# Rolling a matrix by DMA: row copies in long DMAs of shrinking size instead of one row per engine

## The chip, the cores and the metric

The kernel runs on one core of a Trainium2 chip. The metric is the device time of one execution in microseconds (us), the median of several runs. Jobs differ: the median of the kernel before lay between 818 and 832 us in the jobs below (831.87 and 820.19 us in two jobs that both name chip 9), so every comparison is with runs of the kernel before on the same chip in the same rounds.

## The reference

```python
x = np.random.randn(8192, 8192).astype(np.float32)      # 256 MiB
def reference(x, shift):                                 # shift = 100
    return np.roll(x, shift, axis=1)
```

Every row moves 100 columns to the right, and its last 100 elements come to the front. It is a copy: 268.44 MB have to be read from HBM and as much written.

## The kernel before

The output's columns 256 to 8191 (the *rows*, 31,744 bytes each) are copied straight from HBM to HBM, by the issuing queues of SP and ACT in turn. The first 256 columns (the *heads*) go through SBUF, on GpSimd's queue, with two VectorE copies per tile that put the wrapped pieces together.

```python
engines = [nc.sync, nc.scalar]
xm = x.rearrange("(c e j) w -> c j e w", e=16, j=4)
om = out.rearrange("(c e j) w -> c j e w", e=16, j=4)
for c in range(n_rows // 64):              # 128 blocks of 64 rows
    for j in range(4):                     # one row for each of the 16 DMA engines
        engines[j % 2].dma_start(out=om[c, j, :, a:], in_=xm[c, j, :, g:n_cols - s])
# ... heads: 20 loads of HBM into SBUF on GpSimd's queue, 8 VectorE copies ...
for k, h in enumerate(tiles):
    for q in range(Q):
        nc.gpsimd.dma_start(out=ot[k, q, :, :, :a], in_=h[:, q])      # 16 stores
```

Here `s` is 100, `a` is 256 and `g` is 156. Each row DMA gives one row to each engine. The framework keeps four DMAs per issuing queue in flight: the fifth is issued when the first has landed on all 16 engines.

Of the kernel before, what the change touches and what calls it, by code (L numbers as in the profile page):

```python
# [1 line left out]

# [4 lines left out]


@with_exitstack
def kernel(  # L10
    ctx: ExitStack,
    tc: tile.TileContext,
    x: bass.AP,
    shift: int,
    out: bass.AP,
):
    nc = tc.nc
    n_rows, n_cols = x.shape
    s = shift % n_cols
    a = -(-s // 128) * 128  # L20
    if 0 < a <= 384 and a + 128 <= n_cols:
        a += 128
    g = a - s
    P = nc.NUM_PARTITIONS
    engines = [nc.sync, nc.scalar]
    n_chunks = 16
    rows = n_rows // n_chunks





    xm = x.rearrange("(c e j) w -> c j e w", e=16, j=4)
    om = out.rearrange("(c e j) w -> c j e w", e=16, j=4)
    if a < n_cols:
        for c in range(n_rows // 64):
            for j in range(4):
                engines[j % 2].dma_start(out=om[c, j, :, a:], in_=xm[c, j, :, g:n_cols - s])
    if a == 0:
        return  # L40


    if a > 512:
        for i in range(n_chunks):
            r = slice(i * rows, (i + 1) * rows)
            nc.gpsimd.dma_start(out=out[r, :s], in_=x[r, n_cols - s:])
            if g > 0:
                nc.gpsimd.dma_start(out=out[r, s:a], in_=x[r, :g])
        return





    Q, J = 4, 4
    n_st = n_rows // (P * Q * J)
    reads = ctx.enter_context(tc.tile_pool(name="reads", bufs=n_st))
    heads = ctx.enter_context(tc.tile_pool(name="heads", bufs=n_st))
    xt = x.rearrange("(k p j q) c -> k q p j c", q=Q, j=J, p=P)
    ot = out.rearrange("(k p j q) c -> k q p j c", q=Q, j=J, p=P)  # L60
    tiles = []
    for k in range(n_st):
        t = reads.tile([P, Q - 1, J, a], x.dtype)
        h = heads.tile([P, Q, J, a], x.dtype)
        for q in range(1, Q):
            lead = bass.AP(tensor=x.tensor, offset=(k * P * J * Q + q) * n_cols - s,
                           ap=[[J * Q * n_cols, P], [Q * n_cols, J], [1, a]])
            nc.gpsimd.dma_start(out=t[:, q - 1], in_=lead)  # L68
        nc.gpsimd.dma_start(out=h[:, Q - 1, :, :s], in_=xt[k, Q - 1, :, :, n_cols - s:])  # L69
        nc.vector.tensor_copy(h[:, :Q - 1, :, :s], t[:, :, :, :s])  # L70
        if g > 0:
            nc.gpsimd.dma_start(out=h[:, 0, :, s:], in_=xt[k, 0, :, :, :g])  # L72
            nc.vector.tensor_copy(h[:, 1:, :, s:], t[:, :, :, s:])  # L73
        tiles.append(h)
    for k, h in enumerate(tiles):
        for q in range(Q):
            nc.gpsimd.dma_start(out=ot[k, q, :, :, :a], in_=h[:, q])  # L77


# [1 line left out]
_INS = ['x', 'shift']  # L81
_OUTS = [((8192, 8192), 'float32')]

_NUMBERS = {'shift': 100}


# [26 lines left out]
```

## Time and profile before

| | |
|---|---|
| time, median of 3 runs | 821.17 us (819.21 to 822.31) |
| profiled span | 818.3 us |
| share of the engines' time in packets: q1, q10, q0 | 46.0%, 46.4%, 6.8% |
| HBM traffic over the span | 656 GB/s |
| row DMAs, size, time to landing | 512, 496 KB, 12.6 us |
| last head packet over at | 484.9 us |

Whether the 16 DMA engines are the bound, or wait inside their packets for something shared, has to be read from the packets' durations. The prediction does this and shows the lines. In them, a row of 40 digits or numbers stands for 40 equal slices of the span; a digit is the engines' busy share in tenths (9 is 90% or more).

### The profile page before, as it was taken

To read this page: it belongs to the slowest core of one execution; us is meant where nothing else is said; L and a number is where in the kernel's file an instruction comes from. 1 tells how busy PE (TensorE), PEld (TensorE's weight loads), DVE (VectorE), ACT (ScalarE), POOL (GpSimd) and SP (SyncE) were. 2 spreads that over 40 slices of the span, in tenths; PEclk is the share of its full clock that TensorE was granted. 3 is DMA by queue.
4 is the path that set the end of the run, shared out by engine and by line. 5 is a ranking of instruction groups with operands and counts; after the bars stand their busy time and mean duration, and the time that the engine had idled before them with its cause. 6 is when DMAs were issued, how large, how long until landed. Compare 5 with 4: busy or idle time off the path is not lost. (4 is left out here: it accounts for less than half of the span.)

```text
span 818.3 us, 617 instructions
## 1 busy us (share of the span) xinstructions
DVE 7.7 (1%) x8; POOL 28.8 (4%) x40
## 2 busy tenths in 40 slices
DVE  0000000000000000000000000000000000000000
POOL 3000000000000000000000000000000000000000
DMA  9999999999999999999999999999999999999997
GB/s 313 343 345 352 338 352 342 363 338 358 349 342 352 354 355 352 348 364 357 337 335 341 327 335 334 326 332 334 338 337 334 330 334 334 332 327 334 334 321 262
DMA packets 21060, 276.89 MB, mean 338 GB/s; under 512 B 8768, under 2 KB 8768, under 8 KB 12864
## 3 DMA queue, kind: packets, MB, share of 16 engines
q10 hardware_dynamic: 8192, 130.04, 46.4%
q1 hardware_dynamic: 8192, 130.04, 46.0%
q0 software_dynamic: 4672, 16.78, 6.8%
q14 instruction: 4, 0.03, 0.0%
HBM read 268.44 MB, written 268.44 MB: 656 GB/s over the span
## 5 line engine op out<-in xcount | busy, mean ns | idle before, releaser
L77 POOL DMA_DIRECT2D out_dram<-h x16 | 13.2, 825 | 197.8 <-DMA out_dram<-h 112.6
L68 POOL DMA_DIRECT2D t<-in_x_dram x12 | 9.5, 793 | 59.7 <-DMA h<-in_x_dram 30.0
L70 DVE COPY h<-t 128x1200 f32<-128x1200 f32 x4 | 3.1, 786 | 232.3 <-DMA t<-in_x_dram 173.4
L73 DVE COPY h<-t 128x1872 f32<-128x1872 f32 x4 | 4.9, 1224 | 0.0
L69 POOL DMA_DIRECT2D h<-in_x_dram x4 | 3.0, 748 | 45.4 <-DMA t<-in_x_dram 45.4
L72 POOL DMA_DIRECT2D h<-in_x_dram x4 | 3.0, 750 | 41.7 <-DMA t<-in_x_dram 41.7
L94 POOL MEMSET const-float32-0.0<- 128x1 f32 x1 | 0.1, 98 | 0.2 <-issue 0.2
L94 POOL MEMSET const-bfloat16-1.0<- 128x1 bf16 x1 | 0.1, 102 | 0.0
L94 POOL MEMSET const-uint8-127<- 128x1 uint8 x1 | 0.1, 99 | 0.0
L94 POOL MEMSET const-float32-1.0<- 128x1 f32 x1 | 0.1, 98 | 0.0
## 6 DMA issues: line engine op xcount, KB each, us to landing
out_dram<-in_x_dram ACTq DMA_DIRECT2D x256, 496.0 KB, 12.6
out_dram<-in_x_dram SPq DMA_DIRECT2D x256, 496.0 KB, 12.6
out_dram<-h POOLq DMA_DIRECT2D x16, 512.0 KB, 113.7
t<-in_x_dram POOLq DMA_DIRECT2D x12, 512.0 KB, 94.9
h<-in_x_dram POOLq DMA_DIRECT2D x4, 312.0 KB, 92.1
h<-in_x_dram POOLq DMA_DIRECT2D x4, 200.0 KB, 97.4
```

The lines of the kernel that those rows point to most:

```text
L68: nc.gpsimd.dma_start(out=t[:, q - 1], in_=lead)
L69: nc.gpsimd.dma_start(out=h[:, Q - 1, :, :s], in_=xt[k, Q - 1, :, :, n_cols - s:])
L70: nc.vector.tensor_copy(h[:, :Q - 1, :, :s], t[:, :, :, :s])
L72: nc.gpsimd.dma_start(out=h[:, 0, :, s:], in_=xt[k, 0, :, :, :g])
L73: nc.vector.tensor_copy(h[:, 1:, :, s:], t[:, :, :, s:])
L77: nc.gpsimd.dma_start(out=ot[k, q, :, :, :a], in_=h[:, q])
L94: nc = _bacc.Bacc("TRN2", target_bir_lowering=False, num_devices=1)
```

## The change

Its intent is fewer and larger row DMAs. A DMA now holds up to 32 rows per engine; the sizes shrink (32, 24, 18, 13, 10, 7, 6, 4, 3, 2, 2, then 1) so that the end stays fine-grained, and the last four blocks are cut in half rows.

```diff
-    xm = x.rearrange("(c e j) w -> c j e w", e=16, j=4)
-    om = out.rearrange("(c e j) w -> c j e w", e=16, j=4)
-    if a < n_cols:
-        for c in range(n_rows // 64):
-            for j in range(4):
-                engines[j % 2].dma_start(out=om[c, j, :, a:], in_=xm[c, j, :, g:n_cols - s])
+    xm = x.rearrange("(c e j) w -> j e c w", e=16, j=4)
+    om = out.rearrange("(c e j) w -> j e c w", e=16, j=4)
+    blocks = n_rows // 64
+    steps, c = [], 0
+    while c < blocks:
+        steps.append((c, max(1, (blocks - c) // 4)))
+        c += steps[-1][1]
+    for c, n in steps:
+        ways = 2 if c >= blocks - 4 else 1
+        edge = [a + (n_cols - a) * k // ways for k in range(ways + 1)]
+        for j in range(4):
+            for lo, hi in zip(edge, edge[1:]):
+                if lo < hi:
+                    engines[j % 2].dma_start(out=om[j, :, c:c + n, lo:hi], in_=xm[j, :, c:c + n, lo - s:hi - s])
```

The heads' code is the same in both.

## The prediction

> **What bounds the kernel now.** I read the page's slices first, to see which engine is full. Compute is all but idle (VectorE 7.7 us, GpSimd 28.8 us of 818.3), while the row of the DMA engines is full from the first slice to the last but one:
>
> ```profile
> DMA  9999999999999999999999999999999999999997
> GB/s 313 343 345 352 338 352 342 363 338 358 349 342 352 354 355 352 348 364 357 337 335 341 327 335 334 326 332 334 338 337 334 330 334 334 332 327 334 334 321 262
> ```
>
> The reader is to see two stages: some 350 GB/s up to slice 19, some 333 GB/s from slice 20 on, and a short fall at the end. Next, the queues and the memory:
>
> ```profile
> q10 hardware_dynamic: 8192, 130.04, 46.4%
> q1 hardware_dynamic: 8192, 130.04, 46.0%
> q0 software_dynamic: 4672, 16.78, 6.8%
> ...
> HBM read 268.44 MB, written 268.44 MB: 656 GB/s over the span
> ```
>
> q1 and q10 carry the rows (columns 256 to 8191, 31,744 bytes each), q0 carries the heads. Together 99.2% of the 16 engines' time is packets: there is almost no empty time to win. What has to shrink is the time of a packet itself. Third, the stretches of time:
>
> ```profile
> 200.00:300.00 100.00, 1.83 (x2) 6.60 (x8) 1.00 1.01 349
> ...
> 500.00:600.00 100.00, 0.00 (x0) 0.00 (x0) 1.00 1.00 333
> 600.00:700.00 100.00, 0.00 (x0) 0.00 (x0) 1.00 1.00 334
> 700.00:800.00 100.00, 0.00 (x0) 0.00 (x0) 1.00 1.00 329
> 800.00:818.00 18.00, 0.00 (x0) 0.00 (x0) 1.00 0.73 258
> ```
>
> The last column is GB/s through the DMA engines, the one before it their busy share. A row is read from HBM and written to HBM, so from 500 us on HBM sees 2 x 333 = 666 GB/s. From 200 to 300 us the packet records have 4.31 MB of heads, 43 GB/s, which touch HBM only once: 2 x (349 - 43) + 43 = 655 GB/s. Two different mixes, the same HBM traffic within 2%: I take HBM, near 660 GB/s, to be the bound, and not the engines.
>
> The packet records of the trace support this. A row's packet took 1,467 ns in the mean (6,016 + 6,077 us of the two queues, less 74 us of small packets, over 8,192 rows), but never less than 1,173 ns, and about a fifth took 1,173 to 1,180 ns. That floor is 31,744 B / 1.175 us = 27.0 GB/s per engine, 432 GB/s for 16. When engines run out of work at the end, so that 9 or fewer are still busy (after 812 us), every row takes 1,174 to 1,175 ns. With all 16 at work the mean is 1,513 ns. So a row is stretched because the others are there: a shared limit.
>
> Last, the waits of the issuing queue and the issues:
>
> ```profile
> SPq L38 <- DMA out_dram<-in_x_dram: 670.4, 252, 3.9
> ...
> out_dram<-in_x_dram ACTq DMA_DIRECT2D x256, 496.0 KB, 12.6
> out_dram<-in_x_dram SPq DMA_DIRECT2D x256, 496.0 KB, 12.6
> out_dram<-h POOLq DMA_DIRECT2D x16, 512.0 KB, 113.7
> ```
>
> SP waits 252 times out of 256 issues: the first four go out free, each later one waits for the one four before it. So four DMAs per queue, eight rows per engine, are in flight. 670 us of waiting look large but cost nothing, since the engines stay full behind them. The last head packet is over at 484.9 us, 330 us before the end: the heads are off the end's path.
>
> **What the Trainium skill says.** (1) "DMA: Bandwidth & Descriptors", section "Anatomy of one DMA": about 2 us fixed cost per DMA, mostly waiting for the write's receipt, while the semaphore write itself is nearly free. The trace agrees on the second: a completion packet takes 9 ns, and in the bulk-only stretch (490 to 812 us) a row right after completion packets takes 1,512 ns, a row after another row 1,513 ns. (2) The same page, "Queues, rings and completion order": each engine goes round its queues packet by packet. The trace agrees: on an engine a q1 row, a q10 row, and their two completion packets follow each other. (3) The same page, "Rules for kernel authors": at least 1 MiB per DMA for full bandwidth. The rows' DMAs have 496 KB, so the rule speaks for the change; the full engines speak against a gain from it. (4) "HBM Reference", "Specifications (TRN2)": 716 GB/s per HBM domain. The 656 GB/s of this trace are 92% of that.
>
> **The change part by part.** The instruction order shows 44 row DMAs on each of SP and ACT in place of 256: for each of the four row residues j, DMAs of 32, 24, 18, 13, 10, 7, 6, 4, 3, 2, 2 rows per engine, then seven of one row, of which the last four are cut in two halves. GpSimd's and VectorE's lists are the same, so the heads are untouched. Bytes are the same; the descriptors stay one row of 31,744 B, but for 16 rows per engine that become two halves. On an engine the rows are still the 512 rows e x 4 + j of each 64-row block, only in another order.
>
> *Removed: completion packets.* 512 x 16 = 8,192 become 88 x 16 = 1,408. On an engine, q1 row and q10 row abut (the next starts 2 ns before the end), and across the two completion packets the next row starts about 8 ns after the end: a pair costs about 10 ns. 256 pairs: 2.6 us per engine; 83% of it goes, 2.1 us. This is worth its full size only if engines are the bound. Under an HBM bound other rows stretch into it: I count a third, 0.7 us.
>
> *Removed: issues.* 424 issues at 510 to 517 ns are 108 us of sequencer time per queue, all beside full engines: 0 us.
>
> *Moved: the end.* Following each engine's packets by their times, the 16 engines stop between 811.2 and 816.8 us, mean 813.7. Perfect balance would gain 3.1 us. With half rows the last steps in flight are half as long: I count half, 1.5 us, less a little because HBM is less loaded when few engines run (rows at 1,175 rather than 1,513 ns): 1.2 us.
>
> *Moved: how far engines may part.* Now the 16 completions of a DMA come within about 6 us of each other (at most 9.3), since a fifth DMA waits for the slowest engine. With 32 rows per DMA, an engine may lead by dozens of rows. In the first 60 us of the run the spread grew from 0.6 to 5.9 us before it stopped growing, so engines do part. Every engine has the same 512 rows, so a leader stops early or is held back in the small steps, and the laggards then run at the floor. This costs nothing as long as about 12 engines are at work (12 x 27 x 2 = 648 GB/s). I count 0, with an uncertainty of a per cent or so, because another set of rows open at once may suit HBM better or worse.
>
> *Added: descriptor generation of long DMAs.* 512 descriptors in an issue instead of 16. The engine starts on the first while the rest are made: 0 to 1 us at the start.
>
> Sum: 0.7 + 1.2 + 0 - 0.5 = about 1.4 us less, 820. I lean a little further, to 817, because of the two open terms (completions, row order) the first can only gain, up to 1.4 us more, and a change of this shape was presumably kept for a reason.
>
> **Rivals.** *Completions do cost.* If the 292 ns by which the mean row exceeds the floor (1,467 - 1,175) came from one completion per row, long DMAs would remove most of it: 512 x 0.29 = 150 us per engine. HBM at the stated 716 GB/s would stop it at 536.9 MB / 716 = 750 us. For it: 496 KB DMAs and the rule of 1 MiB. Against it: rows after completions are no longer than others, and lone engines with completions run at the floor. 8%, giving 750 to 790 us.
>
> *Row order and HBM.* Stretches come from a shared limit, and that may depend on which rows are open together. In the first 5 us, when engines were still in step, the second row took 1,251 to 1,298 ns on all 16, faster than ever later with 16 at work. So the way the streams lie to each other can matter. With engines further apart it may go either way: 800 to 835 us. 20% for a visible effect.
>
> *The heads starve.* If an engine took a whole DMA of 32 rows as one turn, heads would get one packet per 64 rows, about 95 us, and would be left for the end. Their packets are 890 us in sum, 56 us per engine (41 at the floor, 256 x 160 ns), with the chain read, copy, write behind: 840 to 860 us. The present trace can't exclude it, as each DMA has one row per engine. But a row of 31,744 B is a packet by itself here, and 4 pieces of 1,024 B make one of 4,096 on q0: packets go by size, and I expect rows to stay packets. 5%.
>
> **Range and chances.** The main path gives 815 to 821 us. HBM's reaction widens it to 800 to 828, which should hold 8 times in 10. More than 2% faster means under 804.7: most of the 8% of the first rival, and about a third of the second: 0.15. More than 2% slower means over 837.6: the starving heads and a little of the second: 0.07. The rest, 0.78, is the same.
>
> **What would show it.** Right: completions on q1 and q10 fall from 4,096 to 704 each, the engines' share stays near 99%, HBM stays within 1% of 656 GB/s, rows in the bulk-only stretch stay near 1,500 ns with the same floor, heads still end by 500 us, the last engines stop within some 4 us. Wrong: rows' mean falls toward 1,175 ns (completions or order did cost), rows grow longer (order), the q0 packets run to the end of the span (starving), or engines are empty in the last slices by more than now (they parted and were not brought together). A time under 800 or above 828 would mean that the shared limit is not the fixed 660 GB/s that I read.

## The result

The changed kernel took 825.36 us (823.34 to 826.5, six runs) against 820.99 us (818.13 to 822.31, six runs) for the kernel before. The ratio is 1.0058, with a 95% interval of 1.0037 to 1.0079. A ratio is the mean time of one kernel's runs over that of the other's of the same rounds, so not quite the ratio of the medians. The change costs 0.6%: inside the predicted range, but a loss where a small gain was forecast.

The page of the changed kernel, slices and queues (queue, packets, MB, share of the 16 engines' time):

```profile
DMA  9999999999999999999999999999999999899988
GB/s 312 329 341 343 343 338 342 341 336 336 336 344 341 333 347 341 342 329 345 341 335 338 339 332 344 338 342 340 350 343 343 334 333 342 332 355 339 316 278 301
...
q10 hardware_dynamic: 4928, 130.03, 45.7%
q1 hardware_dynamic: 4928, 130.03, 44.8%
q0 software_dynamic: 4672, 16.78, 7.1%
HBM read 268.44 MB, written 268.44 MB: 651 GB/s over the span
```

Two things are new. The sharp step at slice 20 is gone: the heads, which made it, no longer end there. And the engines are no longer full near the end: the shares add up to 97.6% of a longer span, and the last slices show 8s. Each row queue has 4,928 packets in place of 8,192: completions fell from 4,096 to 704 per queue, as worked out.

The views by stretch, first of the kernel before, then of the changed one. The last two columns are the engines' busy share and their GB/s:

```profile
640.00:700.00 60.00, 0.00 (x0) 0.00 (x0) 1.00 1.01 337
700.00:760.00 60.00, 0.00 (x0) 0.00 (x0) 1.00 1.00 331
760.00:800.00 40.00, 0.00 (x0) 0.00 (x0) 1.00 1.00 326
```

```profile
640.00:700.00 60.00, 0.00 (x0) 1.43 (x2) 1.00 0.97 336
700.00:760.00 60.00, 0.00 (x0) 0.00 (x0) 1.00 0.93 342
760.00:800.00 40.00, 0.00 (x0) 0.00 (x0) 1.00 0.85 303
800.00:825.00 25.00, 0.00 (x0) 0.00 (x0) 1.00 0.82 285
```

Up to 640 us nothing is lost: the changed kernel moves HBM bytes as fast as the other. From there engines run empty, and from 760 us this shows in the rate. (GB/s through the engines is no measure of HBM alone: head bytes touch HBM once, row bytes twice. So I added up HBM bytes from the packet records.)

| from the packet records of the two profiles | before | changed |
|---|---|---|
| span, us | 818.3 | 824.3 |
| time in packets, mean of the 16 engines, us | 811.5 | 804.6 |
| empty time, mean of the 16 engines, us | 6.8 | 19.8 |
| HBM traffic, 60 to 640 us, GB/s | 660.9 | 660.3 |
| HBM traffic, 640 us to the last packet, GB/s | 655.3 | 633.4 |
| time that this costs against the rate of 60 to 640 us, us | 1.5 | 7.5 |

The last row is, for the kernel before, 176.8 us x (1 - 655.3 / 660.9) = 1.5 us, and for the changed one 183.1 us x (1 - 633.4 / 660.3) = 7.5 us. The difference, 6.0 us, is the whole difference of the two spans. (The profiled run of the changed kernel was the slowest of its six; the medians differ by 4.4 us.)

Of the 7.5 us, 5.3 are lost between 770 and 810 us. From 700 to 770 us, with the leading engines idle for much of it, the mean was 14.9 engines at work, and HBM still moved 654 GB/s. From 770 to 810 us it was 13.7 engines and 573 GB/s, and for 8 us of the 40 no more than 11 engines were at work.

**Why engines run empty.** Each DMA leaves 16 completion increments in the trace, one per engine. The time between the first and the last is how far the engines are apart (below: *spread*). For SP's DMAs:

```
rows per engine      first    last    spread, us
32  (1st DMA)        100.3   104.1     3.8
24  (3rd)            264.1   289.8    25.7
13  (7th)            471.8   530.3    58.4
6  (13th)            627.7   702.5    74.8
3  (17th)            710.8   753.8    43.1
1  (23rd)            771.9   785.6    13.7
half (29th)          795.5   801.1     5.5
```

Over all row DMAs the largest spread is 75.9 us; in the kernel before it is 9.3 us. Some engines get through their rows faster than others (why, the runs do not show), and nothing brought them together again until the DMAs became short. Then the leaders waited, because the next short DMA is issued only when the slowest engine has finished the fourth before it. At SP's 23rd DMA two engines completed at 785.4 and 785.6 us, and the other fourteen between 771.9 and 776.9 us: from about there on the fourteen had to wait for the two.

```profile
SPq L46 <- DMA out_dram<-in_x_dram: 681.6, 40, 79.2
...
out_dram<-in_x_dram SPq DMA_DIRECT2D x2, 11904.0 KB, 326.3
...
out_dram<-in_x_dram SPq DMA_DIRECT2D x16, 248.0 KB, 6.0
```

These are the issuing queue's waits (total us, times, longest) and two of its issues (size, us to landing) in the changed kernel. The longest of the 40 waits is 79.2 us, where the longest before was 3.9 us.

**The heads came late.** The issues of the heads' stores in the two kernels (duration, then first and last start in us), before first:

```profile
L77 POOL DMA_DIRECT2D out_dram<-h x16: 711/711/1622, 177.9 to 373.0; - x16
```

```profile
L85 POOL DMA_DIRECT2D out_dram<-h x16: 711/711/1623, 325.3 to 686.5; - x16
```

The last head packet was over at 812.4 us, where it had been 484.9 us. I had expected no change. The order of packets on single engines shows the reason (A, B: a row on q1, on q10; a, b: their completions; H: a head packet), read from the packet records between 120 and 200 us:

```
before    A B H a b H A B H a b H A B H a b H ...
changed   A B H A B H A B H A B H A B H A B H ...
```

An engine goes round its three queues packet by packet, and a completion of 4 bytes is a packet like any other. With one row per DMA, the heads had two turns per two rows; in long DMAs they have one. The completions that I counted as 10 ns of overhead were also giving the heads their turns.

### The profile page after: what moved, and what is told of

It is laid out like the page before. It is cut to its first block, busy times and chain, and to the rows that moved or that the text cites. A ratio compares the mean times of both kernels' runs of the same rounds, so it can differ in the third digit from the quotient of the medians.

```text
span 824.3 us, 193 instructions
## 1 busy us (share of the span) xinstructions
DVE 7.7 (1%) x8; POOL 28.8 (3%) x40
## 3 DMA queue, kind: packets, MB, share of 16 engines
q10 hardware_dynamic: 4928, 130.03, 45.7%
q1 hardware_dynamic: 4928, 130.03, 44.8%
## 4 chain that ended last, share of the span: by engine, by line
another core or an unknown queue 72%; issue 4%; DMA 4%; POOL 3%; POOLq 0%; PEldq 0%
DMA t<-in_x_dram 4%; POOL out_dram L85 2%; POOL t L76 1%; POOL h L80 0%; POOL h L77 0%; POOLq L116 0%; POOLq L85 0%; PEldq L116 0%
```

## The experiments

Theory P: the loss is the lead. Long DMAs let engines part, and the lead has to be repaired, or stands, at the end. Rivals: the half rows leave too little in flight (W), short DMAs cost (S), the row order suits HBM less (O), late heads cost (H). Edits are against the changed kernel unless said otherwise.

**e1_halves_only.** One row per DMA as before; only the last four blocks in halves.

```diff
-        steps.append((c, max(1, (blocks - c) // 4)))
+        steps.append((c, 1))
```

> One part of the change alone: every row DMA has one row per engine as before, only the last four blocks are cut in halves. Theory P (the changed kernel loses because its engines part by up to 75 us and two laggards finish alone): engines stay within about 9 us, so the time is that of before, ratio 0.997 to 1.002, perhaps 1 us better at the end. Rival W (halves make the work in flight too shallow, four half rows per queue): ratio 1.003 to 1.006, engines emptied in the last 25 us as in the changed kernel. Heads end near 485 us as before in both.

Measured: 829.76 us against 831.6 us, ratio 0.9978 (0.9959 to 0.9996). Spread at most 9.8 us, heads end at 492.5 us. The halves are a small gain by themselves, so W falls for halves alone.

**e2_no_halves.** The long DMAs without the halves.

```diff
-        ways = 2 if c >= blocks - 4 else 1
+        ways = 1
```

> The changed kernel without the halves: steps of 32 down to 1 row per engine. Theory P: the spread still grows to about 75 us, the engines are still emptied between 640 and 800 us, ratio to before 1.004 to 1.010. Rival W: the loss is gone, ratio 0.998 to 1.002.

Measured: 839.04 us against 831.6 us, ratio 1.0101 (1.0079 to 1.0124), spread up to 53.4 us (about 75 had been expected). The loss comes with the long DMAs.

**e3_uniform2 and e4_uniform16.** As e2, and all steps of 2 rows, or of 16 rows.

```diff
-        steps.append((c, max(1, (blocks - c) // 4)))
+        steps.append((c, 2))        # e4: 16
```

> All row DMAs have two rows per engine, no halves, no shrinking. Theory P: four DMAs in flight hold the engines within about twice the spread of before, 12 to 18 us; the laggards are that much later at the end, of which a part is lost: ratio 1.002 to 1.010. Theory of turns (an engine goes round its queues packet by packet and a completion counts as one, so heads get a turn per row with one-row DMAs, half a turn per row with long ones): here a head turn per A B, A B, completions, that is three per four rows, so the heads' last packet comes at about 485 / 0.75 = 650 us. Rival to the turns (heads late because GpSimd waits longer): they end near 485 us.

> All row DMAs have sixteen rows per engine, no halves and no shrinking. Theory P: four DMAs in flight let engines part by as much as they like; some 75 us of spread stand at the end, when two engines run alone near the floor of 1,175 ns per row: 840 to 870 us, ratio 1.025 to 1.06. Rival S (it is the short DMAs at the end of the changed kernel that cost): ratio 0.995 to 1.002. Heads by the theory of turns: a turn per two rows, so they end after 800 us.

Measured: e3 1.012 (1.0098 to 1.0142) with a spread of up to 19.1 us; e4 851.1 us, 1.0217 (1.0184 to 1.025), with a spread of up to 71.3 us. Without the shrinking end the lead stands there as a tail. The ratio of e3 is above what I had expected, that of e4 below. Slices of e4:

```profile
DMA  9999999999999999999999999999999999999872
GB/s 309 330 336 341 328 332 344 334 335 331 337 331 334 337 333 335 335 328 330 330 338 322 338 328 337 327 327 335 337 337 330 327 331 335 331 330 338 324 308 115
```

The engines are full for 37 slices and then drop out; the last slice moves a third. S falls as the cause of the loss: a kernel with no short DMA at all is the slowest.

The theory of turns passed a sharp test. It gave three turns per four rows for e3 and so 650 us for the heads' last packet; it came at 650.8 us.

**e8_order_only.** The new row order, in DMAs of one row.

```diff
-    for c, n in steps:
-        ...
+    for c, n in steps:
+        for half in range(2):
+            for k in range(c, c + n):
+                for j in (2 * half, 2 * half + 1):
+                    engines[j % 2].dma_start(out=om[j, :, k, a:], in_=xm[j, :, k, g:n_cols - s])
```

> The changed kernel's row order (on each queue 32 rows of residue 0, then 32 of residue 2, and so on) in DMAs of one row per engine, without halves. It holds the engines within 9 us. Theory P (what costs is that engines part: HBM moves about 1% less with engines far apart, and the laggards end alone): ratio 0.998 to 1.002. Rival O (the order of the rows in memory costs, as HBM likes the old order better): ratio 1.004 or more, with all engines busy and HBM about 1% lower than before in the bulk-only stretch. Heads end near 490 us in both.

Measured: 819.04 us against 818.27 us, ratio 1.0007 (0.9991 to 1.0023), spread at most 8.7 us, heads end at 480.4 us. The order alone costs nothing that shows.

**e9_pairs_in_old_order.** Against the kernel before: two neighbouring issues of one queue become one DMA.

```diff
-    xm = x.rearrange("(c e j) w -> c j e w", e=16, j=4)
+    xm = x.rearrange("(c e i p) w -> c p e i w", e=16, i=2, p=2)     # om alike
-            for j in range(4):
-                engines[j % 2].dma_start(out=om[c, j, :, a:], in_=xm[c, j, :, g:n_cols - s])
+            for p in range(2):
+                engines[p].dma_start(out=om[c, p, :, :, a:], in_=xm[c, p, :, :, g:n_cols - s])
```

> The other half of that pair: the old order of rows, with the two neighbouring issues of a queue joined in one DMA of two rows per engine. Theory P: as the uniform two-row run before it (ratio 1.012): spread 12 to 19 us, ratio 1.008 to 1.015, heads end near 650 us. Rival O: ratio 0.998 to 1.003 in spite of the spread.

Measured: 825.15 us against 818.27 us, ratio 1.0074 (1.0056 to 1.0091), spread up to 20.9 us, heads end at 640.3 us. So joining two rows in one DMA, with nothing else changed, costs at least about as much as the whole change does (the intervals overlap). The heads end 180 us before the end here, so they are not in the way of it.

**e12_pairs_two_in_flight.** As e9, with a DMA of 64 bytes on one engine after each row DMA. It takes one of the four places in flight, so that two row DMAs remain per queue, four rows per engine and queue, as in the kernel before.

```diff
+    tiny = ctx.enter_context(tc.tile_pool(name="tiny", bufs=n_rows // 32))
     for c in range(n_rows // 64):
         for p in range(2):
             engines[p].dma_start(out=om[c, p, :, :, a:], in_=xm[c, p, :, :, g:n_cols - s])
+        for p in range(2):
+            bit = tiny.tile([1, 16], x.dtype)
+            engines[p].dma_start(out=bit, in_=x[0:1, :16])
```

> Two-row DMAs in the old order as in the pair run (ratio 1.0074, spread up to 21 us, heads ending at 640 us), but after each comes a tiny DMA of 64 bytes on one engine, which takes its place among the four in flight: so only two row DMAs, four rows per engine, are in flight per queue, as in the kernel before. The head turns stay those of two-row DMAs. Theory P (parting costs): the spread falls back to about 9 us and the time to that of before, ratio 0.998 to 1.003, while heads still end after 600 us. Rival H (the slower heads, or the missing completions, cost): ratio stays at 1.006 to 1.010.

Measured: 817.39 us against 820.5 us, ratio 0.9961 (0.9949 to 0.9973), spread at most 6.4 us, 3.3 us in the median (20.9 and 16.1 us in e9). The same row DMAs, with added work, turn from a loss into a gain once engines are held together. Slices of e9, then of e12:

```profile
GB/s 314 345 337 339 353 346 343 339 340 344 348 338 354 349 342 353 357 349 345 347 347 354 354 342 350 333 343 336 337 335 331 333 339 328 335 321 342 338 324 147
```

```profile
GB/s 318 335 347 343 346 351 351 353 351 351 342 366 360 352 352 346 357 351 345 353 355 338 338 337 330 330 332 332 324 333 330 340 334 332 329 329 335 336 336 265
```

They differ at the end, 147 against 265 GB/s in the last slice. For 11.3 us of the end of e9 four engines or fewer were at work (8.3 us in its repeat below), in e12 for 0.5 us. By the same sum as above, from 640 us on e9 loses 8.7 us against its own rate, e12 0.9 us. One expectation failed: the heads ended at 519.5 us and not after 600. The packet records show head packets in bursts (H H H H): an engine that waits for its next row now spends the wait on heads.

**e5_before_no_heads and e6_after_no_heads.** Both kernels without heads (a `return` ahead of them; columns 0 to 255 stay unwritten). Their outputs are wrong, which doesn't matter for the times.

> The kernel before without its heads (columns 0 to 255 of the output stay unwritten: wrong on purpose). 520.1 MB of HBM traffic at some 660 GB/s and 6 us for start and end: 794 us, ratio 0.967. It is the base for the next run.

> The changed kernel without its heads (wrong on purpose as well). Theory P with laggards that lag whatever the heads do: the spread still grows to 50 us or more and the run is 3 to 10 us longer than the kernel before without heads. Rival H (late heads cost): both without heads agree within 2 us, in spite of the spread. Rival Q (engines lag because of the heads' queue): both agree and the spread stays under 15 us.

Measured: 790.6 us (789.75 to 791.87; 794 had been expected) and 793.69 us (790.57 to 794.98). The spread still grows, to 58.2 us, so engines part without any heads. The gap, 3.1 us of medians, is smaller than the 4.4 us with heads, and the ranges overlap: in the profiled run of e6, the fastest of its four, HBM still moved 654 GB/s from 660 to 760 us with 15.0 engines at work. So part of the loss may need the heads: in the changed kernel two engines came 8 to 10 us behind all others from about 740 us on, and no such pair is seen here. But a gap of 3.1 us with ranges that overlap does not show it, and how large that part is stays open.

**e14_halves_everywhere.** Every row in two DMAs of half rows, which gives the heads their turns back.

```diff
-        ways = 2 if c >= blocks - 4 else 1
+        ways = 2
```

> The changed kernel with every row cut in two DMAs of half rows. Turns: one head packet per two half rows, as many per row as in the kernel before, so the heads end near 490 us; four DMAs of up to 32 half rows in flight still let engines part by dozens of us. It tells parting from late heads: theory P (parting alone costs): spread over 40 us, ratio 1.003 to 1.008; rival H (late heads are what costs): ratio 0.997 to 1.001.

Measured: 833.1 us against 831.87 us, ratio 1.0015 (0.9998 to 1.0032). The heads end at 475.6 us, as turns predict. But the spread reached only 13.7 us, against my expectation of over 40, so the run doesn't tell the lead from the late heads. It fits both. Why engines part less in half rows is open.

**e7_cap4.** Steps of at most 4 rows.

```diff
-        steps.append((c, max(1, (blocks - c) // 4)))
+        steps.append((c, max(1, min(4, (blocks - c) // 4))))
```

> The changed kernel with its steps capped at 4 rows per engine (4, then 3, 2, 2, 1, and halves). Theory P: the spread is held below about 40 us in place of 76, and the shrinking end has less to repair: ratio 0.999 to 1.004, below the changed kernel's in the same rounds. If the cost belonged to multi-row DMAs as such and not to the lead that they allow, the ratio is that of the changed kernel.

Measured: 840.08 us against 831.87 us, ratio 1.0089 (1.0055 to 1.0122), spread up to 43.8 us, heads end at 780.4 us. A cap of 4 holds the spread down in part but does not help; this expectation failed. The sum from 640 us on finds only 1.0 us here, of the 8.2 us between the medians. The rest lies earlier: HBM moved 642 GB/s from 300 to 600 us with all engines at work, against 654 in the profile of the next run (after_again) on the same chip. So P does not explain this run. It speaks for a cost of multi-row DMAs as such, in this row order at least; where that comes from is open.

**after_again.** The changed kernel on the chip of e7 and e14.

> The changed kernel once more, on the same chip and beside the same runs of before as the three others: 1.003 to 1.008, spread over 60 us, heads ending after 790 us.

Measured: 838.35 us (830.0 to 840.04), ratio 1.0058 (1.0022 to 1.0094): the result repeats on another chip. Its profiled run happened to be the fastest, 830.0 us, and in that run the spread stayed at 29.5 us (over 60 had been expected). The loss from 640 us on is 3.6 us there, against 7.5 us in the slower run on the first chip with its 75.9 us. This is one profile on each of two chips, so a hint that the lead varies and takes the time with it, not more.

**e10_all_halves and e11_adjacent_rows.** Against the kernel before: all rows in halves, or 16 adjacent rows for the 16 engines.

```diff
+        mid = a + (n_cols - a) // 2
         ...
-                engines[j % 2].dma_start(out=om[c, j, :, a:], in_=xm[c, j, :, g:n_cols - s])
+                for lo, hi in ((a, mid), (mid, n_cols)):
+                    engines[j % 2].dma_start(out=om[c, j, :, lo:hi], in_=xm[c, j, :, lo - s:hi - s])
```

```diff
-    xm = x.rearrange("(c e j) w -> c j e w", e=16, j=4)      # om alike
+    xm = x.rearrange("(c j e) w -> c j e w", e=16, j=4)
```

> All rows in halves: 1,024 row DMAs of 248 KB, old order. Theory P continued to the other side: four half rows in flight per queue hold the engines within about 3 us; HBM moves as much as or a little more than with one-row DMAs, and the end is tighter: ratio 0.990 to 1.000. Rival W (too little in flight): engines run empty, ratio 1.01 or more with the engines' share under 97%. Turns: two completions per row, so heads get up to twice the turns per row and end well before 485 us, limited then by GpSimd's waits: 300 to 420 us.

> One-row DMAs as before, but the 16 engines take 16 adjacent rows (32 KB apart) instead of every fourth (128 KB apart). No part of the change: it asks whether the distance of the rows that are open at once moves HBM's rate at all. If the rate loss of parted engines is a matter of which rows are open together, this may differ by 1% or more from before in either direction; if HBM takes any rows alike, ratio 0.997 to 1.003.

Measured: e10 820.55 us, 1.0028 (1.0005 to 1.0051), with a spread of at most 4.2 us: closer than in the kernel before, but no faster. Holding engines closer than one-row DMAs do gives nothing more, against my expectation; why it costs a little was not followed up. e11 822.12 us, 1.0042 (1.002 to 1.0063): taking 16 adjacent rows instead of every fourth does move the time, by a few tenths of a per cent. The heads' stores, first of e3, then of e10, in the same view as above:

```profile
L85 POOL DMA_DIRECT2D out_dram<-h x16: 711/711/1621, 231.5 to 494.1; - x16
```

```profile
L79 POOL DMA_DIRECT2D out_dram<-h x16: 711/711/1622, 77.7 to 145.0; - x16
```

With two completions per row (e10) the heads' last packet was over at 179.9 us, earlier than I had expected (300 to 420), and than the 242 us that twice the turns alone would give, which was not followed up; with three turns per four rows (e3) at 650.8 us. Nothing in the heads' code differs.

**e13_pairs_and_halves.** e12 with the last four blocks in half-row DMAs.

```diff
-    for c in range(n_rows // 64):
+    for c in range(n_rows // 64 - 4):
         ...                                       # pairs, as in e12
+    mid = a + (n_cols - a) // 2
+    for c in range(n_rows // 64 - 4, n_rows // 64):
+        for i in range(2):
+            for lo, hi in ((a, mid), (mid, n_cols)):
+                for p in range(2):
+                    engines[p].dma_start(out=om[c, p, :, i, lo:hi], in_=xm[c, p, :, i, lo - s:hi - s])
```

> A candidate to beat both: two-row DMAs in the old order with two in flight per queue (ratio 0.9961 in its run), and the last four blocks in half-row DMAs (that part alone gave 0.9978). If the two gains add, both being a tighter end: ratio 0.993 to 0.996. If they are the same gain twice: 0.995 to 0.998.

Measured: 828.29 us against 831.87 us, ratio 0.9957 (0.994 to 0.9974), correct. It beats both kernels by a little; against e12 it isn't a difference that these runs can tell.

**e3_again, e9_again and e15_new_order_two_in_flight.** The two-row runs on one chip, and e3 with the tiny DMAs of e12.

> The uniform two-row run again (1.012 on another chip than the old-order pairs, 1.0074), now on the same chip as them. If the row order costs once engines lead: 1.010 to 1.014, and HBM 1% lower between 300 and 600 us than in the old order. If the difference was the chip's: within 0.3% of the old-order pairs.

> Two-row DMAs in the old order again: 1.005 to 1.010, HBM in the middle as in the kernel before, the loss all in the last 60 us.

> Two-row DMAs in the changed kernel's order, held to two in flight by the same tiny DMAs as before. Theory P with the order harmless while engines stay together: spread about 9 us, 0.995 to 0.999 as in the old order. If new order and two rows cost by themselves: 1.003 or more.

Measured: e3 1.0108 (1.0095 to 1.0121), e9 1.0081 (1.0068 to 1.0095), e15 0.9999 (0.9984 to 1.0013). Holding two in flight removes 1.1% in the new order too, with the spread of row DMAs down from 21.2 to 6.8 us at most, and to 3.8 us in the median: P holds a second time. But the gain of e12 did not come (0.995 to 0.999 had been expected). What remains between the orders, about 0.3% on this chip, appears with two-row DMAs and not with one-row DMAs (e8). HBM moved 657 GB/s from 300 to 600 us in e3 and 662 in e9, one profile each. Why is open.

## Why the prediction was wrong

**The bound was right while all engines are at work.** The shared limit is near 660 GB/s of HBM traffic: from 60 to 640 us the two kernels moved 660.9 and 660.3 GB/s with quite different DMAs and a different mix of heads. That also settles the first rival: taking away 83% of the completions moved nothing in this stretch.

**The step that failed** is "how far engines may part", put down as "I count 0, with an uncertainty of a per cent or so". The mechanism was named, that a leader "stops early or is held back in the small steps", but its price was wrong: it cost 6.0 us in the profiled pair, the whole difference of the spans. The reason given, that it "costs nothing as long as about 12 engines are at work", thought of leaders that stop while the others run at the floor. While only the leaders were idle, that was nearly so (700 to 770 us: 14.9 engines, 654 GB/s; in e4 from 790 to 820 us, 13.6 engines and 631 GB/s, against 642 from 640 to 780 us). What was missing is the other case, "held back in the small steps": two laggards stopped the fourteen others at each short DMA. From 780 to 800 us 13.3 engines were at work on average and HBM moved 568 GB/s; only about half of the row packets that started there were at the floor, and the mean is also made of moments with far fewer engines. e9 against e12, the same row DMAs with and without the lead, 1.0074 against 0.9961, shows the price of a lead most cleanly. The prediction had named the sign, engines that are empty in the last slices by more than now, and it came. Its other half did not: the engines were brought together (the completions of SP's last DMA lie within 1.4 us), but that had been paid for on the way. That 825 us lies inside the range of 800 to 828 us is partly luck, since the width was given for HBM's reaction to the rows and not for engines that wait.

**The end.** Half rows were put at a gain of 1.2 us; alone they gave 1.8 us of medians (e1). Right, and far smaller than the loss.

**Completions.** A gain of 0.7 us was counted; none shows apart. e12, with half of the row completions and the engines held together, is 3.1 us faster than the kernel before, but its end is also fuller (0.9 us lost from 640 us on, against 1.5 us), so this gain isn't split. The 2 us of fixed cost per DMA, which the prediction quoted from a section about GpSimd's DMAs, entered no sum, and no run here measures it. One reading of the rows was low: 27% of them, not a fifth, took 1,173 to 1,180 ns. Nothing hangs on it.

**Descriptors of long DMAs.** SP's first row packet started 2.2 us after the span's start (2.1 us before), so the 0 to 1 us was right. New is that one issue instruction lasted up to 69 us on SP and 74 us on ACT (0.6 and 0.8 us before), beside full engines.

**Heads.** "Heads still end by 500 us" failed: 812.4 us. The page on queues was quoted for the packet-by-packet round, and completions were counted as packets, but the two were not put together. The rival in which heads starve had the right direction and the wrong mechanism: rows did stay packets of their own, and what the heads lost were the turns that completions had given them. Its price, 20 us and more, did not come, since the heads still ended before the rows. Whether late heads cost a part of the 6 us is open (e6 hints at some; e14 can't tell).

**Row order.** The second rival is refuted for one-row DMAs (e8: 0.2% at most) and leaves a few tenths of a per cent with two-row DMAs. The lower rate of e7 may belong here too; no run tells.

**The lean from 820 to 817 us** "because a change of this shape was presumably kept for a reason" had no line of the profile behind it. It made a forecast of nothing into a forecast of a gain.

## What to carry to other kernels

Where a shared memory is the bound, as here, larger DMAs saved overhead that cost nothing that showed, but they loosened the tie between the engines: the number of DMAs in flight times the rows in each bounds the lead that one engine may gain (spreads of up to 6.4, 9.3 and 20.9 us with two DMAs of two rows, four of one and four of two), and what stands of it at the end is paid. That is not the whole cost of long DMAs, as e7 shows. If larger DMAs are wanted, keep fewer of them in flight, and look at the first and last completion of each DMA, not only at the engines' mean share. And before taking small packets off a queue, count who shares the engine's rounds with it: they set how fast the other queues move.

## What the Trainium skill lacked or had wrong

- "DMA: Bandwidth & Descriptors", "Queues, rings and completion order", describes the packet-by-packet round but does not say that a 4-byte completion counts as a turn. Here the same heads ended at 179.9, 484.9, 640 to 651 and 812 us with two, one, a half, and hardly any completions per row.
- The same page, "Rules for kernel authors", asks for at least 1 MiB per DMA. For this HBM to HBM copy, 496 KB and up to 15,872 KB moved 660.9 and 660.3 GB/s of HBM traffic from 60 to 640 us; the larger ones lost 0.6%, and plain pairs of 992 KB 0.7 to 0.8%.
- "DMA: Bandwidth & Descriptors" has engines that finish independently, and two that are usually slower, but neither it nor another page says how far the engines of one DMA part when many rows are queued: up to 75.9 us here with long DMAs, 9.3 us with four one-row DMAs in flight per queue. Whether the two laggards here are the two that it names is open, since the packet records do not name the engine.
- "HBM Reference", "Access" and "Specifications (TRN2)", has no figure for one core copying from HBM to HBM, and "DMA: Bandwidth & Descriptors" has rates for copies of other shapes only. The profiles here show 644 to 664 GB/s, read and write together, from 60 to 640 us.
